# Carried blocks' low parts on GpSimd, the pool blocks as a pair with four quads, and three quads a pair in the output product

## The chip, the cores and the metric

The kernel runs on one core of a Trainium2 chip. The metric is the device time of one execution in microseconds; before, the median of three runs was 2002.8 us (2002.09 to 2007.41). Engines are called as in the profile: PE is TensorE's matmul, PEld its weight load, DVE is VectorE, ACT is ScalarE, POOL is GpSimd, SP is SyncE, whose queue starts most DMAs.

## The reference, cut to what matters

One block of 256 tokens and width 2048: a half-weighted SwiGLU feed-forward (5632 wide), a hybrid mixer, and a second feed-forward, each with a norm before and after.

```python
f = _swiglu(_rmsnorm(h, ln_ffn1_pre), ffn1_gate, ffn1_up, ffn1_down)
h = h + 0.5 * _rmsnorm(f, ln_ffn1_post)
mx = _hybrid_mixer(_rmsnorm(h, ln_mix_pre), ...)
h = h + _rmsnorm(mx, ln_mix_post)
f = _swiglu(_rmsnorm(h, ln_ffn2_pre), ffn2_gate, ffn2_up, ffn2_down)
h = h + 0.5 * _rmsnorm(f, ln_ffn2_post)
...
# in the mixer
p = u @ w_in
z_a, z_b, g_a, g_b = jnp.split(p, IN_SPLITS, axis=-1)
y_a = _rwkv7_branch(z_a, ...) @ w_proj_a
y_b = _pool_branch(z_b, pool_w, pool_scale) @ w_proj_b
m = jax.nn.sigmoid(g_a) * y_a + jax.nn.sigmoid(g_b) * y_b
return m @ w_out
```

The RWKV branch is a recurrence over the tokens; the pool branch takes windowed means (2, 4, 8 and 16 tokens) of four groups of 256 columns, each then multiplied by a 256 x 256 matrix.

## The kernel before, in words

**Numbers.** All products keep fp32's accuracy with three matmuls: each operand is split into a high part in `fp32r` (ScalarE copies it, `split`, line 600) and a low part (DVE subtracts, line 602), and `mm3` (line 619) adds high x high, high x low and low x high. A half product below is one `mm3`: 128 rows of the sum, 128 tokens, 512 output columns. Tokens come as two halves `h`. Activations are kept transposed in units of 128 x 1024 (`new_T`, line 749); weights go through rings of five tiles (`w` as it is loaded, `wH`, `wL`), the rest through 34 units (`NUNITS`, tag `u`). PSUM has four banks `mm` (`bank`) and four `pt` (`psum`).

**Quads.** Where two column blocks (f and l, 512 columns each) are multiplied with the same activations, two row blocks of each form a 2 x 2 product that takes seven half products in place of eight, for sums of the weights and of the activations. `Columns` (line 830) does that. In the gate/up blocks a quad comes in two parts: `early` (line 863, four half products, during the block before, with `join`, line 893, after the last one) and `late` (line 882, three). In the products `down` a `quad` (line 905) does all seven, with `merge` (line 929). The weights' sums are DVE's; a quad's fourth sum `t4` has a ring of its own, `hH` and `hL` of 512 columns (`HB`). The activations' sums come from `sums` (line 671) for two quads at a time, made from a tile `sx` that `sums_of` (line 690) adds up from high and low part, or in `normed` (line 1043) from the tile `nx`. `pair` (line 857) multiplies two row blocks of one column block without quads.

**Order.** `ffn` (line 978) runs eleven blocks of 512 hidden columns. A block's f part goes through Silu, its l part is multiplied with it, the result is turned by DVE in 32 x 32 squares (`turn`, line 776), once for each half, and carried through DRAM, which completes the transposition (`carry_raw`, line 781, `carry`, line 799: one DMA out, four back); then ScalarE and DVE split it, half by half. `GATE1` and `GATE2` (lines 50, 51) give the quads of each block, `DOWN1` and `DOWN2` those of the down product's two column pairs (8 and 10). The mixer's order is the string `MIX_ORDER` (line 62): after the block `B0` (gate of the pool branch) come the pool blocks p0 and p1, the decay block l0, k0, r0, the pool matrices m0 to m3, v0, the recurrence `c0` of the first eight heads, and so on; four blocks A (the gate of the RWKV branch); then the product with `w_proj_a`, whose first two column blocks are carried through DRAM too (`MIX_DMA`), and `w_out` by `down` with `OUT_QUADS` (line 52): two quads in each of its two column pairs, the first one after the third pair of rows in the first column pair, after the first in the second. p0 and p1 are two products of their own, without quads, each carried (`tokens`, line 1314) and then windowed (`pool_window`, line 1492).

**Planner.** Every instruction is recorded in program order (`Plan.add`, line 167; so in the profile nearly all have line 499, where they are issued). `cost` (line 215) gives it a price, `deadlines` (line 260) a due time, and `simulate` (line 294) a place: PE keeps the program's order within the streams chain, side and main (chain goes first when it is ready), the other engines take the ready instruction that is due first. A ring's tile is given out in the order of `IN_ORDER` (line 102), when the ring has a free slot. The order that comes out is fixed for each engine before the program runs.

## Time and profile before

| | before |
|---|---|
| runs (us) | 2002.09, 2002.8, 2007.41; median 2002.8 |
| profiled execution, first to last instruction | 2001.8 us, 1.0 under the median of the runs |
| busy: PE, PEld, DVE, ACT, POOL | 99%, 82%, 89%, 59%, 4% |
| TensorE's granted clock | 0.999 |
| DMA | 476.42 MB, mean 238 GB/s |

In the profile a name such as `f<-wL,xH` is the written tile and the tiles read: f and l are the column blocks of a pair, `p` the extra banks of a quad in `down`, `mm` the banks of a single product, `sH` and `sL` the activations' sums, `t` the weights' sums, `T` a turned tile, `x` a carried one. A group's row gives busy us and mean ns of one, then the idle time of its engine just before. A wait's row gives the total us, how often, and the longest. A stage's row gives the length, and for each engine its busy time and number of instructions, then the clock, the share of the DMA engines and GB/s. Gate/up blocks of the first feed-forward lie at about 50 to 450 us, its down product to 690, the mixer to about 1310, the second feed-forward after it.

### The profile page before, as it was taken

To read this page: it belongs to the slowest core of one execution; us is meant where nothing else is said; L and a number is where in the kernel's file an instruction comes from. 1 tells how busy PE (TensorE), PEld (TensorE's weight loads), DVE (VectorE), ACT (ScalarE), POOL (GpSimd) and SP (SyncE) were. 2 spreads that over 40 slices of the span, in tenths; PEclk is the share of its full clock that TensorE was granted. 3 is DMA by queue.
4 is the path that set the end of the run, shared out by engine and by line. 5 is a ranking of instruction groups with operands and counts; after the bars stand their busy time and mean duration, and the time that the engine had idled before them with its cause. 6 is when DMAs were issued, how large, how long until landed. Compare 5 with 4: busy or idle time off the path is not lost.

```text
span 2001.8 us, 28060 instructions
## 1 busy us (share of the span) xinstructions
PE 1990.2 (99%) x9757; PEld 1642.5 (82%) x9757; DVE 1777.1 (89%) x2310; ACT 1177.6 (59%) x1553; POOL 75.0 (4%) x142
## 2 busy tenths in 40 slices
PE   9999999999999999999999999999999999999998
PEld 7888888888888888888888788888888888888887
DVE  8989999999989957898879769898999999998896
ACT  7556556556555756864755355675565665655563
POOL 0000000000000010001300100010000000000000
PEclk9999999999999999999999999999999999999999
DMA  8788888887667887767675477867888888876674
GB/s 278 240 265 263 279 265 282 268 279 222 220 197 251 262 237 232 216 194 221 178 222 172 135 244 224 276 213 244 272 274 262 264 283 273 283 215 215 198 256 148
DMA packets 262558, 476.42 MB, mean 238 GB/s; under 512 B 22800, under 2 KB 50704, under 8 KB 262416
## 3 DMA queue, kind: packets, MB, share of 16 engines
q1 hardware_dynamic: 258752, 464.80, 73.7%
q0 software_dynamic: 3232, 9.44, 1.4%
q8 instruction: 76, 1.25, 0.3%
q14 instruction: 66, 0.54, 0.1%
q10 hardware_dynamic: 432, 0.40, 0.1%
HBM read 446.90 MB, written 26.61 MB: 237 GB/s over the span
## 4 chain that ended last, share of the span: by engine, by line
PE 89%; DVE 5%; DMA 3%; issue 2%; ACT 1%; SPq 0%; POOL 0%; POOLq 0%; DVEq 0%; ACTq 0%
PE l L499 30%; PE f L499 26%; PE mm L499 24%; PE p L499 5%; DVE wL L499 2%; DMA w<-in_ffn_gate_dram 1%; DVE t L499 0%; DMA w<-in_w_out_dram 0%; PE pY L499 0%; DMA w<-in_ffn_up_dram 0%; ACT wH L499 0%; PE tr L499 0%; DVE nx L499 0%; SPq L499 0%; PE pA L499 0%
## 5 line engine op out<-in xcount | busy, mean ns | idle before, releaser
L499 ACT CAST wH<-w 128x1024 fp32r<-128x1024 f32 (+1 forms) x711 | 736.1, 1043 | 617.2 <-PE mm L499 155.1
L499 DVE TENSOR_TENSOR wL<-w,wH 128x1024 fp32r<-128x1024 f32 (+1 forms) x711 | 849.9, 1207 | 146.3 <-ACT wH L499 142.7
L499 PE MATMUL l<-wL,xH 128*128 128x512 f32 x762 | 297.1, 390 | 0.3 <-DVE wL L499 0.2
L499 PE MATMUL l<-wH,xL 128*128 128x512 f32 x762 | 296.8, 389 | 0.0
L499 PE MATMUL l<-wH,xH 128*128 128x512 f32 x762 | 296.7, 389 | 0.0
L499 PE MATMUL f<-wL,xH 128*128 128x512 f32 x652 | 254.1, 390 | 0.3 <-DVE wL L499 0.2
L499 PE MATMUL f<-wH,xH 128*128 128x512 f32 x652 | 253.9, 389 | 0.0
L499 PE MATMUL f<-wH,xL 128*128 128x512 f32 x652 | 253.8, 389 | 0.0
L499 PE MATMUL mm<-wH,xH 128*128 128x512 f32 (+1 forms) x632 | 245.5, 388 | 0.5 <-ACT xH L499 0.5
L499 PE MATMUL mm<-wL,xH 128*128 128x512 f32 (+1 forms) x632 | 244.5, 387 | 1.3 <-DVE wL L499 1.3
L499 PE MATMUL mm<-wH,xL 128*128 128x512 f32 (+1 forms) x632 | 245.0, 388 | 0.0
L499 DVE TENSOR_TENSOR t<-w,w 128x1024 f32<-128x1024 f32 (+1 forms) x162 | 165.2, 1020 | 18.1 <-DMA w<-in_ffn_gate_dram 13.0
L499 PEld LDWEIGHTS l<-wL,xH 128*128 128x128 f32 x762 | 143.1, 188 | 31.3 <-DVE wL L499 1.6
L499 PEld LDWEIGHTS l<-wH,xH 128*128 128x128 f32 x762 | 143.1, 188 | 29.9 <-DVE fg L499 0.3
L499 PEld LDWEIGHTS l<-wH,xL 128*128 128x128 f32 x762 | 143.1, 188 | 29.3
L499 PEld LDWEIGHTS f<-wL,xH 128*128 128x128 f32 x652 | 122.4, 188 | 26.4 <-DVE wL L499 1.1
L499 PEld LDWEIGHTS f<-wH,xH 128*128 128x128 f32 x652 | 122.4, 188 | 25.5
L499 PEld LDWEIGHTS f<-wH,xL 128*128 128x128 f32 x652 | 122.4, 188 | 25.3
L499 PEld LDWEIGHTS mm<-wL,xH 128*128 128x128 f32 x632 | 118.8, 188 | 25.3 <-DVE wL L499 2.6
L499 PEld LDWEIGHTS mm<-wH,xH 128*128 128x128 f32 x632 | 118.8, 188 | 24.5 <-ACT xH L499 0.9
L499 PEld LDWEIGHTS mm<-wH,xL 128*128 128x128 f32 x632 | 118.7, 188 | 23.7 <-DVE xL L499 0.2
L499 DVE TENSOR_TENSOR wL<-t,wH 128x1024 fp32r<-128x1024 f32 x101 | 122.8, 1216 | 6.2 <-ACT wH L499 5.8
(310 smaller groups left out, 2839.4 us busy)
## 6 DMA issues: line engine op xcount, KB each, us to landing
w<-in_w_in_dram SPq DMA_DIRECT2D x128, 512.0 KB, 4.5
w<-in_ffn_up_dram SPq DMA_DIRECT2D x115, 512.0 KB, 4.7
w<-in_ffn_gate_dram SPq DMA_DIRECT2D x111, 512.0 KB, 4.8
w<-in_ffn_down_dram SPq DMA_DIRECT2D x104, 512.0 KB, 4.6
w<-in_ffn_gate_dram SPq DMA_DIRECT2D x191, 256.0 KB, 4.3
w<-in_ffn_up_dram SPq DMA_DIRECT2D x183, 256.0 KB, 4.3
w<-in_ffn_down_dram SPq DMA_DIRECT2D x144, 256.0 KB, 3.9
cx<-T SPq DMA_DIRECT2D x32, 512.0 KB, 3.2
```

Of the source, the lines that this page charges most:

```text
L499: ins = o.fn(*[real(x) for x in o.a], **{n: real(x) for n, x in o.k.items()})
```

## The change

1. Feed-forward blocks: Silu's result is kept in a unit, both halves are turned by one transpose of 1024 columns (`turned`), and the carried tile is split whole, its low part by GpSimd. The planner's price for that on GpSimd is 400 + 2.2 n ns. The mixer's two carried column blocks are turned and split whole too, their low part by DVE.
2. `down` makes the activations' sums from the carried blocks themselves, fetched a second time from DRAM (`raws`, `fetch`: four DMAs), and no longer from high and low part. In `sums` two operations change their form and a ScalarE multiply by -1 is added.
3. The fourth weight sums of a block's quads lie two in a unit and are split together; the ring `hH`, `hL` goes, and `NUNITS` is 36.
4. The first feed-forward's normalised copies start from the raw input, scaled by ScalarE (`scaled`).
5. The mixer's p0 and p1 become one pair, placed after k0, with four quads; their early parts run during k0, in four `pt` banks. The input's sums are made in the step `S`, after B0.
6. `w_out` has three quads in each column pair, from the second pair of rows on in the first column pair.
7. While `w_proj_a` and `w_out` run, weight tiles whose ring is full may take a unit, as long as more than six are free (`LENT`, `KEEP`). The recurrence puts seven of its tiles into others that are no longer used.

```diff
-NUNITS = 34
+NUNITS = 36
...
-OUT_QUADS = ((2, 3, 1.0), (2, 1, 1.0))
+OUT_QUADS = ((3, 2, 1.0), (3, 1, 1.0))
...
-MIX_ORDER = "p0 p1 l0 k0 r0 m0 m1 v0 m2 c0 B1 m3 k1 b0 b1 v1 r1 c1 B2 b2 B3 b3 A0 A1 A2 A3"
+MIX_ORDER = "B0 S l0 k0 p0+p1 r0 m0 m1 v0 m2 c0 B1 m3 k1 b0 b1 v1 r1 c1 B2 b2 B3 b3 A0 A1 A2 A3"
+MIX_QUADS = {"p0+p1": 4}
+MIX_FROM = {"p0+p1": 0.0}
+MIX_TO = 0.8
+MIX_PT = "p0+p1",
+MIX_LEND = "PO"
+MIX_SUMS = 2
...
+LENT = ("w32", "wH", "wL")
+KEEP = 6
+LEND = 0
-IN_ORDER = ("w32", "wH", "wL", "hH", "hL")
+IN_ORDER = ("w32", "wH", "wL")
...
-                if not slots[i.tag] or (i.tag in IN_ORDER and turn[i.tag] != i.seq):
+                if i.tag in IN_ORDER and turn[i.tag] != i.seq:
+                    return False
+                if not slots[i.tag]:
+                    if i.lent and len(slots["u"]) > KEEP:
+                        continue
                     return False
...
+    def tick(s, part):
+        while s.mid and s.mid[0][0] <= part:
+            s.mid.pop(0)[1]()
...
-    def split(s, v, H, L):
+    def split(s, v, H, L, low=None):
         s.nc.scalar.copy(H, v)
-        s.nc.vector.tensor_tensor(out=L, in0=v, in1=H.bitcast(F32), op=ALU.subtract)
+        (low or s.nc.vector).tensor_tensor(out=L, in0=v, in1=H.bitcast(F32), op=ALU.subtract)
...
+    def turned(s, src):
+        T1 = s.unit(p="T1")
+        s.nc.vector.transpose(
+            out=T1.rearrange("p (q m t) -> p m q t", q=4, t=32),
+            in_=src.rearrange("p k h (q t) -> p (k h) q t", q=4))
+        return T1
...
+    def fetch(s, d, m, n):
+        x = s.unit((P, 1024), F32, "x32")[:, :m]
         for q in range(4):
...
-    def carry(s, T1, T, j=None):
-        v = s.carry_raw(T1)
+    def carry(s, T1, T, raws, j=None):
+        x, d = s.carry_raw(T1)
+        low = None
         if j is None:
             T.extend(s.new_T(1))
-            j = -1
...
+            j, low = -1, s.nc.gpsimd
+        raws.append(lambda: s.fetch(d, 1024, 4).rearrange("p (i a b h t) -> p a b h i t",
+                                                          i=4, a=2, b=2, h=2))
+        H, L = [t.rearrange("p k (h c) -> p (k h) c", h=2)
+                .rearrange("p m (i t) -> p i m t", i=4) for t in T[j]]
+        s.split(x.rearrange("p (i m t) -> p i m t", i=4, t=32), H, L, low)
...
-                        s.sums_of(hT[len(sm) // 2], sm)
+                        s.sums(raws[len(sm) // 2](), sm)
...
-        t4, = q.halves(s.t4[k].unsqueeze(1), "h")
+        i = s.quads.index(k)
+        if i % 2 == 0:
+            s.h4 = q.halves(s.t4[i][:, :min(2, len(s.quads) - i)])
...
+        def sums_x():
+            for i in range(MIX_SUMS):
+                x = s.unit((P, 4, S), F32, "sx")
+                uH, uL = [t.rearrange("p k t -> p (k t)").bitcast(F32) for t in uT[i]]
+                nc.vector.tensor_tensor(out=x.rearrange("p k t -> p (k t)"), in0=uH, in1=uL,
+                                        op=ALU.add)
+                s.sums(x.rearrange("p (a b) (h t) -> p a b h t", a=2, h=2), sx)
...
+        def ahead(x):
+            (a, i), (b, j) = [(y[0], int(y[1])) for y in x.split("+")]
+            n = MIX_QUADS[x]
+            J = jobs[x] = Columns(s, w_in, col0[a](i), w_in, col0[b](j), at, NKD, sx,
+                                  [2 * q for q in range(n)],
+                                  s.psum if x in MIX_PT else s.bank)
+            m, out = MIX_FROM[x], []
+            for q in range(n):
+                out.append((m + (MIX_TO - m) * (q + 0.5) / n, lambda k=2 * q: J.early(k)))
+            out.append((out[-1][0], J.join))
+            s.mid = out
...
+        s.plan.lend = "P" in MIX_LEND
         for c in range(4):
             s.gemm_tok(prm["w_proj_a"], c * 512, at_a, NKW, ev_pa(c))
-        s.down(prm["w_out"], s.T_at(mT), NKD, s.post(gpost, 1.0, resid, emit, reload), mT,
-               [], OUT_QUADS)
+        s.plan.lend = "O" in MIX_LEND
+        s.down(prm["w_out"], s.T_at(mT), NKD, s.post(gpost, 1.0, resid, emit, reload), raws,
+               OUT_QUADS)
+        s.plan.lend = False
...
-        pc = reg("pc", 4, S)
+        pc = sw
```

More of the change, by code (lines that the diff above doesn't have):

```diff
@@ L46 @@
 TB = 6
-HB = 2
 AHEAD = 40000.0
@@ L131, in tile @@
         s.tiles[name].kind = name.rsplit("_", 1)[0]
+        s.tiles[name].lent = s.lend and tag in LENT
         return t
@@ L973, in block_seq @@
                 own[pos[i]:pos[i]] = items
-        for fn in own:
+        for i, fn in enumerate(own):
+            s.tick(i / len(own))
             fn()
+        s.tick(1.0)
         ev("l")
@@ L1019, in ffn @@
         su = []
-        nT = s.normed(uT, rb, su, max(quads))
+        nT = s.normed(uT, rb, su, max(quads), xs and xs[4])
         jobs = {}
@@ L1029, in ffn @@
                 s.after.pop(0)()
-            s.block_seq(J, jobs.get(b + 1), evac([1.0, 1.0] if b > 1 else rs, [], J.banks))
-        s.down(wd, s.T_at(hT), NKF, s.post(gpost, 0.5, resid, emit, reload, xs is None), hT, sm,
+            with s.set(lend=b < LEND):
+                s.block_seq(J, jobs.get(b + 1),
+                            evac([1.0, 1.0] if b > 1 else rs, J.banks))
+        s.down(wd, s.T_at(hT), NKF, s.post(gpost, 0.5, resid, emit, reload, xs is None), raws,
                downs)
@@ L1049, in normed @@
             (uH, uL), (nH, nL) = uT[i], nT[i]
-            x = s.unit((P, 4, S), F32, "nx")
-            with s.set(behind=s.late):
-                V.tensor_tensor(out=fl(x), in0=fl(uH).bitcast(F32), in1=fl(uL).bitcast(F32),
-                                op=ALU.add)
+            if raw:
+                x = raw(i)
+            else:
+                x = s.unit((P, 4, S), F32, "nx")
+                with s.set(behind=s.late):
+                    V.tensor_tensor(out=fl(x), in0=fl(uH).bitcast(F32),
+                                    in1=fl(uL).bitcast(F32), op=ALU.add)
             V.tensor_tensor(out=x, in0=x, in1=rb.unsqueeze(1).to_broadcast([P, 4, S]),
@@ new lines, in pair, with ev @@
+        def pair(x):
+            J, evs = jobs[x], {}
+            for b, y in zip("fl", x.split("+")):
+                n = int(y[1])
+                evs[b] = make[y[0]](n, True) if y[0] in make else z_g(y[0], n, True)
+            def ev(b):
+                for h in range(2):
+                    evs[b](h, J.banks[f"{b}{h}"])
+            s.block_seq(J, None, ev)
+        order = MIX_ORDER.split()
+        for x, after in zip(order, order[1:] + [""]):
+            s.plan.lend = x in MIX_LEND
+            n = int(x[1:] or 0) if "+" not in x else 0
+            if "+" in x and x not in jobs:
+                ahead(x)
+                s.tick(1.0)
+            if "+" in after and MIX_FROM[after] < 1:
+                ahead(after)
+            if "+" in x:
+                pair(x)
+            elif x == "S":
+                sums_x()
+            elif x == "B0":
+                s.gemm_tok(w_in, GB, at, NKD, ev_sig(lambda h: sgb0[:, h]), lead=True)
+            elif x[0] == "l":
@@ L1910, in turn, with scaled @@
                                            op0=ALU.mult, op1=ALU.subtract)
+        def scaled(i):
+            with s.set(behind=s.late):
+                for k in range(4):
+                    nc.scalar.activation(out=xT[i][:, k], in_=xT[i][:, k], func=AF.Copy,
+                                         scale=g1[:, 4 * i + k:4 * i + k + 1])
+            return xT[i]
         sq = []
```

206 lines of the change are left out of this document (105 added, 101 removed).

## The prediction

> **What bounds the kernel now.** I read the page's busy shares first, then the chain of work that ended last in order of time, then who makes TensorE wait, then busy time by stage.
>
> ```profile
> span 2001.8 us, 28060 instructions
> PE 1990.2 (99%) x9757; PEld 1642.5 (82%) x9757; DVE 1777.1 (89%) x2310; ACT 1177.6 (59%) x1553; POOL 75.0 (4%) x142
> ...
> 303.05 11.56 PE l L499 x51
> ...
> PE mm L499 <- DVE wL L499: 1.3, 2, 0.8
> PE l L499 <- DVE fg L499: 0.8, 1, 0.8
> ...
> PE pk L499 <- DVE nb L499: 0.4, 1, 0.4
> ...
> PE l L499 <- DVE wL L499: 0.2, 1, 0.2
> PE pB L499 <- DVE AR L499: 0.2, 1, 0.2
> PE f L499 <- DVE wL L499: 0.2, 1, 0.2
> ```
>
> TensorE (PE) is busy for 99% of the span. A busy PE isn't yet PE at its pace, so the third line is the one that counts: 51 matmuls of 512 columns ran in 11.56 us of the chain, 11.56 / 51 = 0.2267 us each. Where PE runs at that pace, only fewer matmuls make the kernel shorter. The waits of PE (total, times, longest) show how little else there is: those that end with VectorE (DVE) sum to 3.1 us. So removed matmuls count in full, as long as DVE, the next engine, keeps up.
>
> ```profile
> core 0: us, PE busy (x) PEld busy (x) DVE busy (x) ACT busy (x) POOL busy (x), PEclk, DMA share, GB/s
> 200.00:440.00 240.00, 240.00 (x1059) 198.45 (x1058) 226.83 (x256) 143.91 (x175) 0.00 (x0) 1.00 0.85 275
> 470.00:690.00 220.00, 220.00 (x972) 182.23 (x971) 202.17 (x228) 130.62 (x146) 4.10 (x25) 1.00 0.73 232
> 700.00:800.00 100.00, 100.00 (x488) 85.02 (x487) 66.51 (x133) 56.31 (x101) 10.45 (x23) 1.00 0.80 236
> 1150.00:1180.00 30.00, 30.00 (x134) 24.84 (x133) 18.68 (x23) 17.86 (x24) 0.00 (x0) 1.00 0.73 241
> 1180.00:1220.00 40.00, 40.00 (x181) 32.92 (x179) 34.77 (x46) 18.93 (x21) 0.00 (x0) 1.00 0.83 251
> 1220.00:1310.00 90.00, 89.20 (x404) 73.50 (x404) 82.97 (x112) 57.68 (x89) 4.30 (x7) 1.00 0.75 248
> 1310.00:1360.00 50.00, 50.00 (x227) 41.32 (x226) 48.60 (x71) 30.55 (x50) 3.40 (x5) 1.00 0.69 219
> ```
>
> The rows are the gate/up blocks, the first down product, the mixer's beginning (pool, decay and key blocks), the A blocks' end, the product with `w_proj_a`, the one with `w_out`, and the second feed-forward's head. DVE is at 226.83 / 240 = 95% in the first and at 92% under `w_out`; only the mixer's beginning has room (66.51 of 100). The clock is full throughout.
>
> How close DVE comes is read from single instructions, DVE's `wL` above the PE matmul that uses it:
>
> ```profile
> 288.28 1.28 DVE L499 TENSOR_TENSOR xL<-x,xH 128x512 fp32r<-128x512 f32 x2
> 291.42 1.22 DVE L499 TENSOR_TENSOR wL<-w,wH 128x1024 fp32r<-128x1024 f32 x1
> 292.69 0.50 PE L499 MATMUL l<-wL,xH 128*128 128x512 f32 x1
> ...
> 1589.66 1.22 DVE L499 TENSOR_TENSOR wL<-w,wH 128x1024 fp32r<-128x1024 f32 x1
> 1590.93 0.51 PE L499 MATMUL l<-wL,xH 128*128 128x512 f32 x1 [0.21 <-DVE wL L499]
> ```
>
> `wL` is done at 292.64 and used at 292.69, done at 1590.88 and used at 1590.93. At these points, just where the next block's quads begin, DVE leads by 0.05 us: any delay there becomes PE idle time, any relief goes unseen or removes 0.2 us.
>
> **The change part by part.** *Matmuls removed.* A quad does seven half products in place of eight, three matmuls each, so it saves three. Four quads in the pool pair and one more in each of the two column pairs of `w_out`: 6 x 3 = 18 matmuls, 18 x 0.2267 = 4.1 us. Nothing else of the change adds or removes a matmul. This is the one term that is on the path by itself; everything below matters only where DVE gets late.
>
> *DVE's prices* (count, busy, mean ns):
>
> ```profile
> L499 DVE TENSOR_TENSOR wL<-w,wH 128x1024 fp32r<-128x1024 f32 x693 | 835.9, 1218 | 134.1 <-ACT wH L499 130.6
> L499 DVE TENSOR_TENSOR t<-w,w 128x1024 f32<-128x1024 f32 x101 | 123.1, 1219 | 16.3 <-DMA w<-in_ffn_gate_dram 13.0 <-DMA w<-in_w_out_dram 1.5 <-DMA w<-in_ffn_down_dram 1.4
> L499 DVE TENSOR_TENSOR w<-w,t 128x512 f32<-128x512 f32 x101 | 69.1, 684 | 0.4
> L499 DVE TENSOR_TENSOR hL<-t,hH 128x512 fp32r<-128x512 f32 x101 | 69.1, 684 | 0.0
> L499 DVE TENSOR_TENSOR xL<-x,xH 128x512 fp32r<-128x512 f32 x48 | 30.9, 684 | 4.0 <-ACT xH L499 4.0
> L499 DVE STREAM_TRANSPOSE T<-sg 128x512 f32<-128x512 f32 x44 | 28.5, 685 | 0.0
> L499 DVE TENSOR_TENSOR sL<-sf,sH 128x1024 fp32r<-128x1024 f32 x15 | 18.2, 1217 | 0.0
> L499 DVE TENSOR_TENSOR sx<-xH,xL 128x1024 f32<-128x1024 f32 x11 | 13.4, 1219 | 0.0
> L499 DVE TENSOR_TENSOR f<-f,s 128x512 f32<-128x512 f32 x18 | 12.4, 690 | 0.0
> L499 DVE SCALAR_TENSOR_TENSOR sf<-sx 128x256 f32<-128x256 f32 x11 | 4.6, 420 | 0.1
> L499 DVE STREAM_TRANSPOSE vt<-zv 128x1024 f32<-128x1024 f32 x2 | 2.5, 1243 | 0.0
> ```
>
> *Feed-forward carries.* Each of the 22 blocks now costs DVE two transposes and two low parts of 512 columns, 2 x 0.685 + 2 x 0.684 = 2.74 us (44 / 2 blocks; 48 low parts with the mixer's four). After: one transpose of 1024, 1.24 by the `vt` row, and the low part of 1024 columns on GpSimd (POOL). POOL has hardly any other work there, and its result is used only in the down product, tens of us later, so its own duration costs nothing; the question is what it does to DVE.
>
> ```profile
> 934.72 1.22 DVE L499 TENSOR_TENSOR wL<-w,wH 128x1024 fp32r<-128x1024 f32 x1
> 934.86 1.35 POOL L499 COPY Z<-ev 64x256 f32<-64x256 f32 x1 [7.17 <-DVE T L499]
> ...
> 945.47 0.39 POOL L499 COPY Z<-ev 64x256 f32<-64x256 f32 x1 [3.97 <-PE pS L499]
> ...
> 633.11 2.70 POOL L499 TENSOR_SCALAR_AFFINE_SELECT mz<-mz 64x64 f32<-64x64 f32 x4
> ...
> 634.99 0.72 DVE L499 TENSOR_TENSOR hL<-t,hH 128x512 fp32r<-128x512 f32 x1
> ```
>
> A POOL copy that began 0.14 us into a DVE subtract of two SBUF tiles took 1.35 us in place of 0.39: it waited till about the subtract's end. The other way round, a DVE subtract beside four POOL selects took 0.72, 0.04 us over its mean, so DVE was hardly held; but those read only 64 elements. The trace has no long two-input POOL operation. Its length, from the nearest row: four times the 256-column copy is 1.6 us, and two inputs at one at a time 3.1; I take the middle, 2.3. While it reads, DVE's two-input operations, nearly all of them here, may stand still for 0 to 2.3 us. A block's DVE time thus changes by 1.24 - 2.74 = -1.5 us (not held) to +0.8 us (held throughout). The copy's wait speaks for the second end, the select's neighbour for the first, and I keep both.
>
> The Trainium skill, "SBUF — State Buffer", section "Who interferes with whom", speaks against this part: a VectorE instruction with two SBUF inputs and a GpSimd instruction that reads SBUF exclude each other for the whole of the one that began first. The copy's row agrees; no row shows VectorE as the one that waits long. "GPSIMD Engine Reference" of the Trainium skill, section "3.1 Elementwise — side-by-side cycle accounting", gives 4497 ns for an add of 2048 fp32 columns on GpSimd, so some 2.25 us here, an estimate; by it the 22 blocks would ask 22 x (2.25 - 1.5) = 16.5 us more of VectorE rather than 33 less.
>
> *Other relief.* Low parts of the fourth weight sums go two at a time (1.22 in place of 2 x 0.684, once or twice a block: 0.15 to 0.3 us). The down products drop ten `sx` sums, 12 us over 2 x 220; in their place come four fetch DMAs each on SP's queue, 0.5 MB a set, 2.6 MB in a stage that moves 232 GB/s x 220 us = 51 MB, ahead of that quad's weights. SP waits there for a free unit, and weight loads queue behind it; the share of the DMA engines is 0.73, and I count nothing. The first feed-forward's normalised copies get four scalings on ScalarE (16 short ones) for four DVE sums; ScalarE is at 59%. Each set of sums also gains one short ScalarE multiply.
>
> *The pool pair.* A quad's DVE work: `t` 1.22, `w` 0.68, `t4` 0.68, three low parts 3.65, half of a paired low part 0.61, in all 6.84, in place of two plain tiles, 2.44. Four: 17.6 more. The join's four adds 2.8. The two input sums 2 x (1.22 + 4 x 0.42 + 1.22) = 8.2. Together 28.6 us, into a stage that leaves 33.5 idle in 100. ScalarE casts as many more high parts; it is busy 56.31 of 100 here and 57.68 of 90 under `w_out`. The stage's bursts: the key block with the four early halves has (96 + 48) x 0.2267 = 32.6 us of PE and asks 8 x 1.22 + 4 x 5.02 + 2.8 = 32.6 us of DVE. That is even, with the plain tiles' lead before it; the pair's second half is light. The bound is 0 to about 5 us of stall (the decay block's evacuation on top); I take 0, the row of 66.51 being nearest. The pair holds all four `pt` banks from the key block until its end; the chain `c0`, which uses them, needs `v0`, two blocks later, and its result only in `w_proj_a`. Blocks `m0` to `m3` wait for the pair's columns; a 22 us block (96 x 0.2267) stands between.
>
> *`w_out`.* Two quads more: 2 x (6.92 - 2.44) = 9.0; two sets of sums without `sx`, 5.8, for one with it, 4.1; the mixer's two carries 0.6 less. Net +10.1 us on DVE. `w_out` itself has 90 - 83.0 = 7.0 idle, `w_proj_a` 5.2, the next head 1.4, less 1.4 of PE saved: 12.2, just enough; the A blocks' last 30 us hold another 11.3, which lent units (fetching and splitting ahead where over six are free) let DVE use. Bound: 0 to 10.1 - 5.6 = 4.5 us. I take 0, since the lending reaches into the emptiest row.
>
> Sum on the profiled span: 2001.8 - 4.1 = 1997.7. The median of the runs is 2002.8, 1.0 over the span, so 1998.7 us. What this kernel can tell from no change is about 0.3%, 6.0 us: faster means under 1996.8, slower over 2008.8.
>
> **The rivals.** *Relief shows.* If POOL doesn't hold DVE, each block gains 1.5 us at the very points with 0.05 us of lead (at 288.28 the two `xL` stand in front of the late `wL`), and the 3.1 us of waits behind DVE go too: 2002.8 - 7.2 = 1995.6. For it: the rows of 292 and 1590; against: the select row is too short to prove it, and `w_out` gets heavier, not lighter. Chance 0.24.
>
> *GpSimd holds VectorE at the quads' start.* POOL starts whenever its high part is there, and the carried tile lands near the next block's first quad (288.28). Held 2.3 us, less the 1.22 of `xL` that are gone and 0.05 of lead, PE stalls 1.0 us. There are 18 blocks that begin with quads ahead; in half of them it makes 2002.8 - 4.1 + 9 = 2007.7. From five on the kernel is slower than before, from eleven by over 0.3%. For it: the copy that waited; against: PE waited behind DVE for only 3.1 us in all, so most blocks have more lead than these two points, and DVE has 5% to catch up. Chance 0.14, 0.09 of it over 2008.8.
>
> *VectorE becomes the bound under the mixer's quads or `w_out`.* Up to 5 and 4.5 us; half of both gives 2003.5, no measurable change. For it: 98% of DVE over those stages; against: their idle neighbours. Chance 0.12.
>
> *The saved matmuls don't show*, because the chain's small matmuls fall otherwise among the large: about 2002.8. Chance 0.05.
>
> **How the numbers follow.** The forecast, matmuls alone and stalls as they are, has 0.45. Faster is the relief, 0.24. Slower is 0.09, from the held cases. The rest, 0.67, is within 0.3%. The range takes in the relief, with 1 us for the chain's order (1994.5), and the held cases to a little short of half (2006.0); some 0.15 lies outside.
>
> **What would show it.** Right: 18 matmuls of 512 columns fewer at the same 0.2267 us; PE's waits for DVE near 3 us; `p` and `f` products with `sH` in the mixer's beginning; `sx` down from eleven to two. The low parts on POOL should take 1.6 to 3.1 us; if DVE operations beside them begin late by that much, and PE then waits for `wL`, the second rival holds. Waits of PE around the key block or under `w_out` show the third. Wrong altogether: a matmul count that did not fall, or PE waits on DMA in the down products behind the second fetches.

## The result and the profile after

The change makes the kernel slower: 2023.9 us (median of five runs, 2019.1 to 2028.9) against 2004.8 for the kernel before beside it, a ratio of 1.0104 [1.0093, 1.0115]. (The ratios and their 95% intervals are the record's; they aren't the quotient of two medians, which is 1.0095 here.) The span of the profiled execution is 2024.1 us, 22.3 more than before. The forecast was 1998.7 us, with a range up to 2006.0.

The page after, first its busy shares, then the shares of the chain that ended last:

```profile
span 2024.1 us, 28233 instructions
PE 1996.8 (99%) x9739; PEld 1638.4 (81%) x9739; DVE 1806.2 (89%) x2248; ACT 1199.2 (59%) x1553; POOL 133.9 (7%) x164
...
PE 13%; DVE 7%; DMA 3%; issue 3%; ACT 3%; SPq 1%; ACTq 0%; DVEq 0%; POOLq 0%; POOL 0%
```

The 18 matmuls are gone (9757 to 9739), and yet PE shows the same 99%: its busy time is no measure of its pace. The shares of the chain here sum to far less than the span (before, PE alone stood for 89%): the view doesn't follow this run back to its start, so nothing is built on it. The waits of PE after (total, times, longest) say more:

```profile
PE l L515 <- DVE wL L515: 11.6, 15, 1.0
PE l L515 <- ACT wH L515: 3.9, 9, 1.3
PE f L515 <- DVE wL L515: 2.1, 4, 0.7
```

Those that end with DVE's `wL` were 0.2 and 0.2 us before. They are many and short: 15 of `l`, none over 1.0 us. Where they lie is seen from the matmuls in a stretch: in the gate/up blocks nearly every matmul has 512 columns and 340 us hold 340 / 0.2267 = 1500 of them. The windows of before (first fence) and of after (second), columns as in the prediction:

```profile
110.00:450.00 340.00, 340.00 (x1500) 281.28 (x1499) 317.95 (x353) 203.74 (x246) 0.00 (x0) 1.00 0.86 273
...
1150.00:1350.00 200.00, 199.20 (x898) 164.29 (x897) 175.63 (x238) 120.80 (x179) 7.70 (x12) 1.00 0.75 241
1370.00:1740.00 370.00, 369.57 (x1626) 304.69 (x1625) 346.06 (x387) 220.35 (x265) 0.00 (x0) 1.00 0.84 269
```

```profile
110.00:450.00 340.00, 334.07 (x1455) 271.98 (x1455) 310.72 (x308) 196.30 (x219) 20.77 (x8) 1.00 0.83 266
...
1150.00:1350.00 200.00, 199.44 (x898) 164.22 (x897) 176.47 (x234) 121.60 (x179) 7.49 (x12) 1.00 0.75 248
1370.00:1740.00 370.00, 362.73 (x1581) 295.63 (x1579) 336.35 (x328) 209.07 (x232) 22.30 (x9) 1.00 0.80 260
```

The first and the third row are the gate/up blocks of the two feed-forwards. Before, PE ran there at its full pace or nearly so (370 us hold 1632). After, 45 matmuls are missing in each: 90 x 0.2267 = 20.4 us. The middle row holds `w_proj_a` and `w_out`, with three quads a pair now: 898 matmuls, as before. The rest of the loss lies in three other windows of after, the key block with the pair's early halves and the beginnings of the two down products:

```profile
735.00:775.00 40.00, 37.70 (x182) 31.57 (x181) 33.20 (x40) 26.15 (x40) 5.16 (x11) 0.96 0.84 253
505.00:535.00 30.00, 28.73 (x126) 23.12 (x125) 27.06 (x32) 18.61 (x22) 0.00 (x0) 1.00 0.74 227
1795.00:1825.00 30.00, 29.33 (x130) 23.97 (x129) 26.33 (x28) 16.42 (x18) 2.41 (x1) 1.00 0.83 230
```

Before, PE was busy for all of the mixer's beginning (160.00 us of 690 to 850). After, it idles for 2.3 us of these 40; by the gaps between one matmul's start and the next one's, over 0.2267, that stage loses 4.5 us. Some 1.6 of them aren't waiting: the granted clock was 0.50 for 3.4 us there (the mean of the stretch is 0.96), and the matmuls in it start 0.43 us apart. The two others held 134 matmuls before: 8 and 4 are missing, 2.7 us. So 20.4 + 4.5 + 2.7 - 18 x 0.2267 = 23.5, against 22.3 measured; where the 1.2 us between them lie isn't shown (in the start and the recurrence the matmuls have other sizes and can't be counted so).

What POOL does to DVE is seen in one place of after, in order of time (start, length):

```profile
1513.70 1.04 ACT L515 CAST xH<-x 128x1024 fp32r<-128x1024 f32 x1
...
1514.82 2.40 POOL L515 TENSOR_TENSOR xL<-x,xH 128x1024 fp32r<-128x1024 f32 x1 [36.47 <-ACT xH L515]
1514.83 3.47 DVE L515 TENSOR_TENSOR t<-w,w 128x1024 f32<-128x1024 f32 x1
...
1518.34 0.69 DVE L515 TENSOR_TENSOR w<-w,t 128x512 f32<-128x512 f32 x1
...
1519.19 1.05 ACT L515 CAST wH<-w 128x1024 fp32r<-128x1024 f32 x1 [4.45 <-DVE w L515]
...
1520.27 1.23 DVE L515 TENSOR_TENSOR wL<-w,wH 128x1024 fp32r<-128x1024 f32 x1 [0.52 <-ACT wH L515]
1520.29 0.51 PE L515 MATMUL l<-wH,xH 128*128 128x512 f32 x1 [0.35 <-ACT wH L515]
...
1521.55 0.50 PE L515 MATMUL l<-wL,xH 128*128 128x512 f32 x1 [0.76 <-DVE wL L515]
```

The carried tile's high part is ready at 1514.74, POOL starts its subtract at 1514.82, and DVE's `t`, which starts 0.01 us later, takes 3.47 us in place of 1.22. It ends at 1518.30, 1.08 us after POOL: so it did nearly all of its work when POOL was through. The delay then runs down a quad's chain, `t`, `w`, ACT's `wH`, DVE's `wL`, and about 5 us after the collision PE stands, first for `wH`, then for `wL`. The same is seen 22 times: in every block one DVE instruction starts beside POOL's and ends 1.08 us after it (0.55 where it has 512 columns). A stall of 1 to 2 us follows within 10 us in 14 of the 22 blocks, 21 us in all, and one of 0.8 and 0.9 us in two more.

### The profile page after: what moved, and what is told of

The parts are those of the page before. It is cut to its first block, busy times and chain, and to the rows that moved or that the text cites. A ratio compares the mean times of both kernels' runs of the same rounds, so it can differ in the third digit from the quotient of the medians.

```text
span 2024.1 us, 28233 instructions
## 1 busy us (share of the span) xinstructions
PE 1996.8 (99%) x9739; PEld 1638.4 (81%) x9739; DVE 1806.2 (89%) x2248; ACT 1199.2 (59%) x1553; POOL 133.9 (7%) x164
## 5 line engine op out<-in xcount | busy, mean ns | idle before, releaser
L515 PE MATMUL l<-wL,xH 128*128 128x512 f32 x849 | 332.4, 392 | 11.7 <-DVE wL L515 11.6
L515 PE MATMUL l<-wH,xH 128*128 128x512 f32 x849 | 331.8, 391 | 4.1 <-ACT wH L515 3.9
L515 PE MATMUL l<-wH,xL 128*128 128x512 f32 x849 | 330.6, 389 | 0.0
L515 DVE TENSOR_TENSOR t<-w,w 128x1024 f32<-128x1024 f32 (+1 forms) x172 | 194.7, 1132 | 29.1 <-DMA w<-in_ffn_down_dram 11.8
L515 PE MATMUL mm<-wH,xL 128*128 128x512 f32 (+1 forms) x568 | 220.2, 388 | 0.0
L515 PE MATMUL mm<-wH,xH 128*128 128x512 f32 (+1 forms) x568 | 219.8, 387 | 0.2 <-ACT xH L515 0.2
L515 PE MATMUL mm<-wL,xH 128*128 128x512 f32 (+1 forms) x568 | 219.8, 387 | 0.1
L515 PEld LDWEIGHTS l<-wL,xH 128*128 128x128 f32 x849 | 159.5, 188 | 49.5 <-DVE wL L515 17.1
L515 ACT CAST wH<-t 128x1024 fp32r<-128x1024 f32 (+1 forms) x144 | 147.3, 1023 | 74.7 <-PE f L515 27.8
L515 DVE TENSOR_TENSOR wL<-t,wH 128x1024 fp32r<-128x1024 f32 (+1 forms) x144 | 170.6, 1184 | 10.1 <-ACT wH L515 6.6
```

Of the source, the lines that this page charges most:

```text
L515: ins = o.fn(*[real(x) for x in o.a], **{n: real(x) for n, x in o.k.items()})
```

## The experiments

Theory H: GpSimd's subtracts hold DVE while they read SBUF, and DVE has no lead at the quads. Rival F: the loss comes from the other edits (fetches twice, paired fourth sums, whole turns and splits), and GpSimd only stands beside it. Rival P: it comes from the pool pair. A ratio below is against the kernel before on the same chip.

**Lows back on DVE (e1), and lows on GpSimd alone (e2).**

```diff
# e1, from after
-            j, low = -1, s.nc.gpsimd
+            j = -1
# e2, from before: two low parts of 512 a block
-            s.split(v[:, :, h], H, L)
+            s.split(v[:, :, h], H, L, s.nc.gpsimd)
```

> The changed kernel, but the carried feed-forward blocks' low parts are made by VectorE again (one subtract of 1024 columns a block); all else of the change stays. Theory (GpSimd's subtract holds VectorE's two-input instructions until it ends): no VectorE subtract over 1.3 us beside it, PE's waits in the gate/up blocks fall from some 23 us to about 2, time 2023.9 - 21 = about 2003 us. Rival (the stalls come from the other edits in those blocks: the whole turn, the paired fourth sums, the new order that the planner makes): they stay, 2018 to 2026 us.

> The kernel before, with one edit: the low parts of the carried feed-forward blocks (two of 512 columns a block) go to GpSimd. Theory: each holds VectorE for some 1.3 us, twice a block at the points where VectorE's lead was 0.05 us, less 1.2 us of work that VectorE loses: slower by 8 to 20 us, 2012 to 2024 us, with VectorE subtracts of 1.5 us and more beside GpSimd's. Rival (other edits): VectorE is relieved, 2000 to 2005 us.

e1 took 2007.3 us, 1.0023 [1.0013, 1.0032]; 16.6 us below the changed kernel's median. e2 took 2021.7, 1.0093 [1.0077, 1.011]; 19.9 above before. The gate/up windows of e1, then of e2:

```profile
110.00:450.00 340.00, 338.22 (x1487) 278.35 (x1486) 313.77 (x321) 201.30 (x226) 0.00 (x0) 1.00 0.85 272
...
1370.00:1740.00 370.00, 367.77 (x1616) 302.29 (x1615) 342.13 (x350) 215.76 (x241) 0.00 (x0) 1.00 0.83 268
```

```profile
110.00:450.00 340.00, 332.65 (x1457) 272.48 (x1456) 309.93 (x329) 196.56 (x240) 28.15 (x16) 1.00 0.83 265
...
1370.00:1740.00 370.00, 364.39 (x1586) 299.20 (x1585) 336.01 (x351) 212.70 (x257) 31.62 (x18) 0.99 0.82 261
```

Without GpSimd's low parts, 13 + 10 matmuls are missing in place of 45 + 45; with nothing but them, 43 + 40, or 18.8 of e2's 19.9 us. One line carries most of the loss in both directions. H holds, P and F can only stand for what is left in e1: some 5.2 us in the gate/up blocks and the pair's stall. A rival that no run takes apart is the planner, which makes a new order for each kernel; but the edits of e7, e10 and e14 (below) change the order too and move the time by 1.5 to 3.2 us from e1, not by 17 to 20.

**Reading, writing, and shorter pieces (e3, e4, e9).** In e3 and e4 DVE makes the low parts and GpSimd gets work whose result nobody uses: a memset of the same 1024 columns, or a sum of high and low part.

```diff
# e3, from e1, after the carried split
+            s.nc.gpsimd.memset(x, 0.0)
# e4, from e1, same place
+            s.nc.gpsimd.tensor_tensor(out=x, in0=H, in1=L, op=ALU.add)
# e9, from after
-        (low or s.nc.vector).tensor_tensor(out=L, in0=v, in1=H.bitcast(F32), op=ALU.subtract)
+            for i in range(4):
+                low.tensor_tensor(out=L[:, i], in0=v[:, i], in1=H[:, i].bitcast(F32), op=ALU.subtract)
```

> As the run with the low parts on VectorE, and GpSimd fills the carried tile with zeros after it was split (1024 columns, nothing read, nobody waits for it). If only GpSimd's reading holds VectorE: as that run, within 2 us, VectorE's subtracts beside the fill at 1.22 us. If any long GpSimd instruction does: VectorE subtracts beside it longer by up to 1 us, time 5 to 10 us over that run.

> As the run with the low parts on VectorE, and GpSimd adds high and low part of each carried block into a dead tile (1024 columns, two inputs, nobody waits for it). Theory: each add takes 2.4 to 2.5 us and a VectorE two-input instruction beside it ends with it (2.7 to 3.4 us in place of 1.22); VectorE keeps its own subtract too, so PE's stalls are at least those of the changed kernel: 2020 to 2040 us. Rival (other edits): as that run, within 2 us.

> The changed kernel, with GpSimd's low part of a carried block cut into four subtracts of 256 columns. Theory (held for each whole instruction, and released between): VectorE's instructions beside them are held some 0.6 to 0.8 us each in place of up to 2.2 once, the sum stays near 2.4 us a block, so PE's stalls shrink at most by a third: 2015 to 2026 us. Rival (only the one long hold does harm, since the plan catches up short ones): 2005 to 2010 us, as with the low parts on VectorE.

e3 took 2005.9 us, 1.002 [1.001, 1.0029], as e1; e4 2046.3, 1.0216 [1.019, 1.0241], 39 over e1; e9 2016.8, 1.0076 [1.0059, 1.0093]. GpSimd's groups in the four kernels, after, e3, e4 and e9:

```profile
L515 POOL TENSOR_TENSOR xL<-x,xH 128x1024 fp32r<-128x1024 f32 x22 | 59.4, 2699 | 878.8 <-ACT xH L515 481.2 <-DMA w<-in_ffn_gate_dram 227.0 <-DVE wL L515 47.1
```

```profile
L515 POOL MEMSET x<- 128x1024 f32 x22 | 21.1, 958 | 899.9 <-DMA w<-in_ffn_up_dram 546.8 <-DVE xL L515 239.8 <-DMA x<-cx 70.3
```

```profile
L515 POOL TENSOR_TENSOR x<-xH,xL 128x1024 f32<-128x1024 f32 x22 | 69.1, 3141 | 894.2 <-DVE xL L515 375.7 <-DMA w<-in_ffn_up_dram 333.3 <-DMA w<-in_ffn_gate_dram 85.7
```

```profile
L515 POOL TENSOR_TENSOR xL<-x,xH 128x256 fp32r<-128x256 f32 x88 | 111.5, 1296 | 825.5 <-ACT xH L515 706.1 <-DMA w<-in_ffn_gate_dram 79.1 <-PE f L515 40.3
```

As many columns written by GpSimd, beside the same work of DVE, cost nothing; read, they cost 39 us. The memset is shorter (0.96 us), but DVE's instructions beside all 22 of them took 1.22 or 0.69 us, as elsewhere, while beside each of e4's 22 sums one was held. So it is GpSimd's reading that holds DVE, not that GpSimd works or writes. e4 loses more than the changed kernel does: it keeps the low parts on DVE, and its sum is longer than the subtract (means 3.14 and 2.70 us). It also ran seven times for 3.4 us at half clock (after: once), which is some 12 us of PE's time. How much of the rest each makes isn't told apart. What DVE lost is read from its groups, in e1 first, then after:

```profile
L515 DVE TENSOR_TENSOR wL<-w,wH 128x1024 fp32r<-128x1024 f32 x694 | 835.8, 1219 | 121.4 <-ACT wH L515 113.7 <-PE f L515 2.6 <-PE l L515 0.5
L515 DVE TENSOR_TENSOR t<-w,w 128x1024 f32<-128x1024 f32 x107 | 130.5, 1220 | 14.3 <-DMA w<-in_ffn_gate_dram 5.8 <-DMA w<-in_ffn_down_dram 4.3 <-DMA w<-in_w_in_dram 3.9
L515 DVE TENSOR_TENSOR w<-w,t 128x512 f32<-128x512 f32 x107 | 73.5, 687 | 1.2
L515 DVE TENSOR_TENSOR t<-w,w 128x512 f32<-128x512 f32 x65 | 44.9, 691 | 2.0
L515 DVE TENSOR_TENSOR xL<-x,xH 128x1024 fp32r<-128x1024 f32 x24 | 29.3, 1219 | 0.0
```

```profile
L515 DVE TENSOR_TENSOR wL<-w,wH 128x1024 fp32r<-128x1024 f32 x694 | 847.5, 1235 | 120.8 <-ACT wH L515 111.7 <-PE f L515 2.6 <-DMA w<-in_ffn_gate_dram 1.1
L515 DVE TENSOR_TENSOR t<-w,w 128x1024 f32<-128x1024 f32 x107 | 147.8, 1381 | 27.4 <-DMA w<-in_ffn_down_dram 11.8 <-DMA w<-in_ffn_gate_dram 5.9 <-DMA w<-in_w_in_dram 5.6
L515 DVE TENSOR_TENSOR w<-w,t 128x512 f32<-128x512 f32 x107 | 77.5, 725 | 1.2
L515 DVE TENSOR_TENSOR t<-w,w 128x512 f32<-128x512 f32 x65 | 46.9, 721 | 1.7
```

The time held, in these four groups: 11.7 + 17.3 + 4.0 + 2.0 = 35.0 us, or 1.59 us a block; `t`, the first step of a quad's chain, is hit hardest (its mean rises by 13%). The 22 low parts that went over were 22 x 1.219 = 26.8 us. DVE gives away less than it loses.

e9 cuts the subtract so that DVE may come in between. Its four pieces took 4.26 us together in one block and 5.66 in another, with DVE's operations beside the latter at 1.58 and 1.76 us in place of 1.22; 36 + 31 matmuls are missing in the gate/up blocks, 23 fewer than after. Shorter pieces share the loss out and cure a quarter of it (23 of 90 matmuls, 5.2 us; 7.1 between the medians). DVE's time beside GpSimd, over what the same instructions take elsewhere, is still 32 us in all (36 after).

**The pool pair (e5, e6, e8, e11).** All from e1 or its kin, so without GpSimd's low parts. e5 puts the pool blocks back as two single products, with the rest of the change as it is; e6 moves the pair behind `r0`; e8 is e6 with e7's edit (below); e11 is e10 (below) with the pair behind `r0` and the pool matrices after `c0` and `B1`.

```diff
# e5
+MIX_ORDER = "B0 p0 p1 l0 k0 r0 m0 m1 v0 m2 c0 B1 m3 k1 b0 ...
# e6
+MIX_ORDER = "B0 S l0 k0 r0 p0+p1 v0 m0 m1 m2 c0 B1 m3 k1 b0 ...
# e11
+MIX_ORDER = "B0 S l0 k0 r0 p0+p1 v0 c0 B1 m0 m1 m2 m3 k1 b0 ...
```

> The changed kernel with the low parts on VectorE, and p0 and p1 as single products without quads, ahead of the decay block, as they were before. Theory (the pair's early halves, the input's sums and the decay block's evacuation overload VectorE between 735 and 775 us, and PE waits there): the 3.7 us of PE stalls around the key block go and 12 matmuls (2.7 us) come back, so 1 us less than the run with the low parts on VectorE, about 2006 us. Rival (the pair pays for itself, the rest is lost elsewhere): 2.7 us more, about 2010 us.

> The changed kernel with the low parts on VectorE, and the pair placed one block later: the early halves run during r0, then the pair, then v0, then m0, m1 and m2. Theory (the stall is the meeting of the early halves with the decay block's evacuation and the input's sums): the 3.7 us of PE stalls go, the 12 matmuls stay saved, about 2003.5 us. Rival (four early halves in one block are too much for VectorE wherever they stand): stalls of 3 us and more move with them, about 2007 us.

> Both edits of the two runs before this one: low parts on VectorE, due 48 us later, and the pair one block later. If each theory holds, their gains add: 2007.3 - 3.7 - 4.5 = about 1999 us, under the kernel before by some 3 us. If neither does, 2007 us.

> As the run before, and the pair one block later, with the block B1 between v0 and m0 so that the pool windows have 22 us more: the early halves run during r0, then the pair, v0, c0, B1, m0 to m3. Theory: neither the stall at the early halves (3.7 us) nor the 5 us wait of the pool matrices for their windows: 3 us less than the run before, about 2000 us. Rival (the load on VectorE only moves): as the run before, within 1.5 us, or over.

e5 took 2007.7 us, 1.0025 [1.0015, 1.0034]: the same as e1 with its pair. The key block, with the decay block's end, in e1 and then in e5, where it comes 44.5 us later:

```profile
735.00:775.00 40.00, 38.44 (x162) 31.12 (x161) 36.08 (x43) 27.31 (x42) 0.84 (x2) 0.96 0.84 258
```

```profile
779.50:819.50 40.00, 40.00 (x186) 33.55 (x185) 31.45 (x62) 26.99 (x49) 0.00 (x0) 1.00 0.80 240
```

With the pair, DVE is busy for 36.08 of 40 us, and PE idles; without, PE is full. By the gaps between starts PE loses 3.7 us there in e1. Only some 2 of them are waiting; then the granted clock falls to half:

```profile
759.00:762.50 3.50, 1.94 (x8) 1.09 (x7) 3.43 (x6) 3.50 (x5) 0.00 (x0) 1.00 0.53 150
762.50:765.90 3.40, 3.40 (x9) 2.65 (x9) 3.40 (x5) 3.40 (x6) 0.00 (x0) 0.50 0.73 181
```

Nine matmuls in 3.40 us, 0.43 us apart, cost another 1.6. So in e1 the burst costs about what the pair's twelve matmuls save, 2.7 us. It need not: e18 (below) has the same pair, no stretch at half clock, and loses 0.4 us in that block. e6 gives the burst more room (its stall falls to 1.3 us), yet took 2011.8, 1.0042 [1.0027, 1.0057]: the pool matrices now come before their windows are made. Its new wait of PE:

```profile
PE mc L515 <- ACT mxT L515: 2.8, 1, 2.8
```

e8 took 2016.8, 1.0067 [1.0052, 1.0082], and e11, which moves the matrices out of the way as well, 2029.7, 1.0145 [1.013, 1.016]: its stretch 850 to 1150, the recurrence, has PE busy for 287.5 of 300 us in place of e1's 299.6, and 17 of the 300 at half clock, which is 8.5 us of its loss. None of e6, e8 and e11 makes the pair pay.

**What is left in the gate/up blocks (e7, e10, e13, e14, e15, e18, e19).** e1 still misses 23 matmuls there. Two ideas and both together: the carried block's low part, now in one piece of 1.22 us, stands in front of a `wL` (e7: let it wait up to 60 us; e14: turn and split half by half as before); the paired fourth sums hold two slots of the `wH`/`wL` ring (e10: give them units of their own; e13: split each alone, in a ring of its own and with 34 units, as before); the two returns to before at once (e15 = e13 + e14).

```diff
# e7
-        s.split(x.rearrange("p (i m t) -> p i m t", i=4, t=32), H, L, low)
+        with s.set(lag=60000.0):
+            s.split(x.rearrange("p (i m t) -> p i m t", i=4, t=32), H, L, low)
# e10
-            s.h4 = q.halves(s.t4[i][:, :m])
+            H, L = [q.unit((P, 2, 512), F32R, n) for n in ("hH", "hL")]
+            q.split(s.t4[i][:, :m], H[:, :m], L[:, :m])
# e13 (e18: one unit h4 for both, and NUNITS = 36)
+        hH, hL = [q.tile(q.wp, [P, 512], F32R, "h" + n, "h" + n, 2) for n in "HL"]
+        q.split(s.t4[i - i % 2][:, i % 2], hH, hL)
# e14
+        for h in range(2):
+            H, L = [t.rearrange("p k (h i t) -> p h i k t", h=2, i=4)[:, h] for t in T[j]]
+            s.split(x.rearrange("p (i k h t) -> p h i k t", i=4, h=2, t=32)[:, h], H, L, low)
```

> The changed kernel with the low parts on VectorE, and the planner's due time for splitting a carried feed-forward block 48 us later (lag 60 us in place of 12), since only the down product needs it. Theory (a 1.22 us subtract that stands in VectorE's queue just before a block's first quad is what PE waits for): PE's stalls in the gate/up blocks fall from 7 us to under 2, about 2002 to 2004 us. Rival (those stalls come from the weights' landing, whatever stands in the queue): no change, 2006 to 2008 us.

> The changed kernel with the low parts on VectorE, and the paired fourth sums split into units of their own in place of a tile of the weights' ring of five. Theory (that tile is held from one late half to the next but one, so that the ring is four deep there and VectorE's lead is less): PE's stalls in the gate/up blocks fall from 7 us to about 2 to 3, time about 2003 us. Rival (the ring isn't short; the stalls come from the order, or from loads that land later): 2006 to 2009 us.

> The changed kernel with the low parts on VectorE, and each fourth sum split by itself in a ring of its own again (512 columns; 34 units). Theory (paired, the sums no longer fill VectorE's wait of 0.5 us for ScalarE's high part just before a block's quads): the stalls in the gate/up blocks fall from 7 us to about 3, about 2003 us. Rival (the other edits of those blocks): 2006 to 2009 us.

> The changed kernel with the low parts on VectorE, and each carried block turned and split half by half again (two instructions of 512 columns each). Theory (a whole turn of 1.24 us and a whole low part of 1.22 us stand before more urgent work, where halves could be put apart): stalls in the gate/up blocks fall from 7 us to about 3, about 2003 us. Rival (the paired fourth sums): 2006 to 2009 us.

> Both edits of the two runs before this one, so that the gate/up blocks are nearly those of the kernel before. If these edits are what is left of the slowdown there: stalls of about 2 us, and only the pair's 3.7 us remain against the 4.1 us of matmuls saved, about 2002 us, as the kernel before. If not: 2006 to 2009 us.

| | median us | ratio | matmuls, 110 to 450 | 1370 to 1740 | PE busy, 850 to 1150 |
|---|---|---|---|---|---|
| before (its profile) | | | 1500 | 1626 | 299.2 |
| e1 | 2007.3 | 1.0023 [1.0013, 1.0032] | 1487 | 1616 | 299.6 |
| e7 | 2010.5 | 1.0041 [1.0026, 1.0057] | 1470 | 1612 | 299.5 |
| e10 | 2009.5 | 1.0044 [1.0029, 1.0059] | 1481 | 1617 | 296.5 |
| e13 | 2020.8 | 1.0085 [1.0065, 1.0104] | 1480 | 1623 | 290.4 |
| e14 | 2008.9 | 1.0032 [1.0022, 1.0042] | 1486 | 1620 | 299.6 |
| e15 | 2012.6 | 1.0053 [1.0036, 1.007] | 1500 | 1634 | 288.6 |

These counts scatter: e1 and e5 differ in the mixer alone, and the first column is 1487 in the one and 1473 in the other, 3.2 us. Beyond that, e7 is worse in both columns and e10 no better, so neither "the low part stands in front" nor "the ring is short" is borne out. e13 and e14 singly change little; e15, both, has no stall left in either feed-forward. But e13 and e15 lose it again in the recurrence. They have two units fewer than e1, and the next kernel gives these back; e19 asks whether half of the pair's quads is better then.

```diff
# e18, from e15
-NUNITS = 34
+NUNITS = 36
# e19, from e18
-MIX_QUADS = {"p0+p1": 4}
+MIX_QUADS = {"p0+p1": 2}
-MIX_SUMS = 2
+MIX_SUMS = 1
```

> As the run with both edits of the gate/up blocks undone, but the fourth sums' halves lie in units, so that 36 units stay (34 there). Theory (whole turns and low parts together with paired fourth sums make the stalls in the gate/up blocks; the 12 us of new stalls between 850 and 1150 us in that run came from its two units less): under 1 us of stalls in the gate/up blocks, 9 us between 850 and 1150 us as before, the pair's 2 to 4 us stay: about 2000 to 2002 us. Rival (the recurrence's order got worse for another reason): 2008 to 2014 us.

> As the run before, with two quads in the pool pair in place of four and one set of input sums: 6 matmuls (1.4 us) more, 13 us less for VectorE around the key block. If the pair's stall is VectorE's overload there: it goes (2 to 4 us), about 1999 to 2001 us. If not: 1.4 us over the run before.

The gate/up blocks and the recurrence in e15, then in e18:

```profile
110.00:450.00 340.00, 340.00 (x1500) 281.06 (x1499) 316.89 (x353) 204.48 (x249) 0.00 (x0) 1.00 0.85 275
...
850.00:1150.00 300.00, 288.64 (x1950) 235.53 (x1949) 245.12 (x430) 156.56 (x238) 35.57 (x59) 0.97 0.62 183
```

```profile
110.00:450.00 340.00, 338.23 (x1488) 278.67 (x1487) 314.58 (x351) 201.70 (x246) 0.00 (x0) 1.00 0.86 273
...
850.00:1150.00 300.00, 299.64 (x2218) 244.24 (x2217) 265.57 (x483) 168.15 (x264) 39.86 (x65) 1.00 0.64 187
```

e18 took 2003.2 us, 1.001 [1.0001, 1.0018]: the recurrence is whole again, so e15's 11 us there come from the two units (or from where the fourth sums lie; e18 changes both). Not all of them are waiting: the clock column says 0.97, for 17 of the 300 us ran at half clock after PE had waited 3 us and more, some 8.5 us of its time. In the gate/up blocks that profile has 12 matmuls fewer than before in the first feed-forward and 2 more in the second (1628). e19 took 2004.5, 1.0009 [1.0, 1.0018], the same. So the whole turns and splits and the paired fourth sums together cost at most a few us: e15 has none of e1's gate/up stalls, while e1 and e18 lie 1.0023 and 1.001 above before with intervals that overlap. How the two edits act together stays open.

**`w_out` (e12, e16).** e12 puts the three quads a pair into before and nothing else; e16 adds the lending of units (`LENT`, `KEEP`, in both products).

```diff
-OUT_QUADS = ((2, 3, 1.0), (2, 1, 1.0))
+OUT_QUADS = ((3, 2, 1.0), (3, 1, 1.0))
# e16 also
+LENT = ("w32", "wH", "wL")
+KEEP = 6
```

> The kernel before with only the three quads in each column pair of w_out (the first after the second pair of rows), its sums still from high and low part and no lending. Prediction's bound: six matmuls fewer, 1.4 us; VectorE has 11 us more work in a stage that left 7 idle, so between 2001 us (covered) and 2006 us (not covered).

> The kernel before with the lending of units to weight tiles during w_proj_a and w_out, and the three quads; nothing else of the change. Theory (the 13 us that the three quads cost alone are VectorE's lateness, and the lending lets it run ahead in the 11 us that were idle before w_proj_a): the stalls of 1200 to 1350 us fall from 18.7 us to about 3, time 2000 to 2002 us. Rival (the lending helps little; it is the carried blocks fetched a second time that relieve VectorE there): 2008 to 2014 us.

e12 took 2015.2 us, 1.007 [1.0055, 1.0085]; e16 2002.8, 1.0001 [0.9991, 1.001]. PE's longest waits for DVE in e12, then the stretch 1150 to 1350 in e12 and in e16, to be read beside the 199.20 of before:

```profile
PE l L499 <- DVE fg L499: 5.3, 1, 5.3
PE mm L499 <- DVE kL L499: 2.8, 2, 2.3
PE p L499 <- DVE xL L499: 2.3, 1, 2.3
```

```profile
1150.00:1350.00 200.00, 189.56 (x827) 155.05 (x826) 172.97 (x240) 117.10 (x176) 9.10 (x12) 0.97 0.69 225
```

```profile
1150.00:1350.00 200.00, 199.11 (x896) 163.79 (x895) 188.58 (x256) 122.99 (x183) 7.48 (x12) 1.00 0.72 240
```

Without lending, the extra DVE work makes PE wait for DVE at the seam to the next feed-forward (`fg`, `xL`); e12's PE is busy for 189.6 us of these 200, and 13.7 of them ran at half clock after the long waits, some 6.8 of its 13 us. With lending, DVE gets more done in the stretch (188.6 us busy, 173.0 in e12) and nothing is late.

## Why the prediction was wrong

*The matmuls* were right: 18 fewer, at the same pace where nothing stalls (1500 in 340 us in e15 too). But even e18, which has all of the 4.1 us and no low part on GpSimd, ends 1.1 us above before: by the gaps between starts it loses 2.5 us more than before in the first gate/up blocks and 1.0 in the mixer's beginning.

*The carries' term failed.* The prediction bounded a block's change of DVE time by -1.5 and +0.8 us, said of POOL's low part that "its own duration costs nothing", and left the carries out of its sum. GpSimd's part in them cost 16.6 us (after against e1) to 19.9 us (e2 against before). Its prices were right: the transpose takes 1.24 us as forecast (x22, 1238 ns), POOL's subtract 2.40 against a forecast of 2.3, and a block's DVE time changed by 1.24 + 1.59 - 2.74 = +0.1 us, inside the bounds. In the first gate/up stretch DVE's busy time per matmul is the same within 1% (310.7 us for 1455, 317.9 for 1500 before). What failed is the step from that sum to the time: nothing in sum is not nothing on the path. DVE's work used to be pieces of hardly over 1.22 us in an order fixed beforehand by prices; now, once a block, one of them takes 1.9 to 3.5 us, which that order doesn't know of, at the quads, where the prediction's own rows showed 0.05 us of lead. The delay then reaches PE through the chain `t`, `w`, `wH`, `wL`.

*The second rival was the right mechanism, undersized.* It had GpSimd hold DVE at the quads' start, at 1.0 us in half of 18 blocks, 2007.7 us. Measured: stalls of 1 to 2 us in 14 blocks, 1.5 on the mean, so both the count and the size were too small. All 18 blocks at its 1.0 us would have given 2016.7. The evidence against it, "PE waited behind DVE for only 3.1 us in all, so most blocks have more lead than these two points", was a wrong inference: a sum of waits near zero says that the lead is enough for the work as it is, not how much is left. Waiting and lead are different things, and the two places at which the lead could be read both said 0.05. Even that is too much: where PE does wait for `wL` (1590.93 before, 1521.55 after), the matmul also starts 0.05 us after the subtract's end, so 0.05 is the hand-over alone, and the lead was nil. The select beside which DVE went on (64 elements) was no test of a long read of two tiles, and should have carried no weight against the copy that waited.

The Trainium skill, "SBUF — State Buffer", section "Who interferes with whom", says that a VectorE instruction with two SBUF inputs and a reading GpSimd instruction shut each other out for the whole of the one that began first; the 3.47 us of `t` beside 2.40 us of POOL agree, and so does the memset that held nothing. The prediction's estimate by the figure of the Trainium skill's "GPSIMD Engine Reference", section "3.1 Elementwise — side-by-side cycle accounting", 16.5 us more of VectorE, is close to the time lost, but by chance: over the carries VectorE's sum changed by some 2 us (22 x 0.1).

*The pair* was bounded by 0 to 5 us and taken at 0; PE loses 4.5 us in its block after and 3.7 in e1, some 1.6 of each at half clock, but 0.4 in e18. So the bound was right, and whether the pair pays hangs on how DVE's other work falls around it. The prediction's own count, 32.6 us of DVE work against 32.6 of PE, left no margin for that.

*`w_out`* was taken at 0, and that is what came (898 matmuls before and after), for the reason given: e12 without lending loses 13 us (2015.2 against 2001.9), about half of them lost to the half clock, well over the bound of 4.5, and e16 with it nothing. The bound was made from idle sums again, and had no term for the clock.

*The second fetches* were counted at nothing. In e1, which has them, the windows at 505 and 1795 hold 134 matmuls each as before; after lost 2.7 us there, with DVE's `t` waiting 2.0 us for a weight tile at 516 and POOL's subtract of 2.41 us in the other window. So the fetches alone cost nothing that shows; why the first window lost in after is not settled.

*Relief shows* did not happen: e3 and e1, with full transposes, fewer `sx` sums (two left, as forecast) and no hold, are 1.002 and 1.0023.

None of the kernels beats the one before by what can be told. e16 equals it at 1.0001 [0.9991, 1.001] and e18 lies within 0.3%; six matmuls saved in `w_out` are 1.4 us, too little to be seen.

## What to carry to other kernels

Before work is moved to an idle engine, ask what that engine's instruction shuts out while it runs, and how long the longest undisturbed piece of the busy engine is against the lead at the place where the moved work will land; the busy sums can balance to 0.1 us a block while the kernel loses 20 us. Little waiting doesn't mean much lead: read the lead, as the distance from the end of the producer to the start of its user, at the places in question; 0.05 us, seen here also where PE waited, is no lead. And a cut elsewhere that frees few matmuls (18, 4.1 us) is worth less than one stall per block. Where PE does wait, look at the granted clock just behind: in e1 a wait of some 2 us was followed by 1.6 us of slow matmuls.

## What the runs showed of the hardware

The hold of DVE by GpSimd is by whole instruction and by reading: beside a subtract of 2.40 us a DVE subtract took 3.47, beside a memset of 0.96 us of the same 1024 columns the means of `t` and `wL` stayed at 1.22. Which forms of reading hold it, beyond two SBUF tiles, no run here asks. It works both ways: GpSimd's subtract, 2.40 us undisturbed, has a mean of 2.70, and one of 256 columns, about 0.73 undisturbed, a mean of 1.30 in e9. Cutting an instruction in four therefore did not give DVE back its time; it made both engines take turns.

A matmul's busy time went on showing 99% while PE lost 22 us, because each matmul is counted for 0.39 us and starts 0.23 us after the one before it; matmuls counted in a stretch of one shape showed the loss at once.

The granted clock can fall after a wait. In e1, e4, e12 and e15 PE idled for 1.6 to 3.6 us within 7 us, and then the clock was 0.50 for 3.4 us or two or three times that, with matmuls 0.43 us apart in place of 0.23. It isn't idle time alone: in e15 PE idled for 2.8 us before 890 us and no such stretch followed, and in e7 one came at 994 us after hardly any idle time (0.1 us). What decides it these runs don't show.
